# Moving deferred sums, row squares and a small rotary table to other places of a decoder-layer kernel

## The chip, the cores and the metric

One core of one Trainium2 chip runs the whole program. The metric is the device time of one execution in microseconds (us); lower is better. The kernel before took 886.24 us (median of 3 runs, 885.25 to 886.32).

## What is computed

One layer of a hybrid decoder. The input is a sequence of 2048 rows of 1024 numbers, with 16 learned "meta" rows put in front. The rows are normalised and projected to eight parts of 512 columns; half of the layer is a gated short convolution (four groups of 128 columns), half is chunked retention (four heads of 128 columns). The mixed result is projected back and normalised.

```python
hn = rms_norm(h, norm_g)
proj = jnp.einsum('bld,de->ble', hn, w_in)
cx, cb, cc, cg, q, k, v, rg = jnp.split(proj, N_PROJ, axis=-1)
conv_out = short_conv_branch(cx, cb, cc, conv_w) * jax.nn.silu(cg)
qf = rotary(q.reshape(shp), pos) * (RET_HEAD_DIM ** -0.5)
kf = rotary(k.reshape(shp), pos)
ret = head_group_norm(retention_chunkwise(qf, kf, vf), ret_norm_g)
ret_out = ret * jax.nn.silu(rg)
h = h + jnp.einsum('ble,ed->bld', jnp.concatenate([conv_out, ret_out], axis=-1), w_out)
```

The 16 meta rows matter only as the state with which a head's retention starts and as the first two inputs of a convolution.

## The kernel before, in words

The sequence is worked in two halves of 1024 rows (`r` = 0 and 1; here: first and second half), then comes the output projection, eight pairs of row tiles. A half consists of eight **units**: unit 0 to 3 are the retention heads (`head`, L623), unit 4 to 7 the convolution groups (`conv_group`, L530; the very first is `group_plain`). `UNITS` (L37) gives their order: 4, 0, 1, 2, 3, 5, 6, 7 in the first half, 0 to 7 in the second.

A unit makes two **quads** (`quad`, L210). A quad multiplies a 2 by 2 block matrix of weights with one of activations by seven products instead of eight (a Strassen form), and each product is 12 matmuls of 128x512, since every operand is split in a high and a low part (L104 on ScalarE casts the high part `wh`, L116 on VectorE subtracts to get the low part `wl`). The weight parts have three buffers each (`RING`), so the cast for a product can start when the product three before it has ended. Three copies on ScalarE (L228, tag `tc`, four buffers) take partial results out of PSUM, after the products 0, 2 and 3; `copied[0]` names the last of them. GpSimd makes the sums of weight blocks (L138 to L141, shown under the helpers' lines L113 and L116).

A head's first quad gives its keys and values, the second its queries and gates. `rotary` (L583) turns keys and queries with four VectorE instructions, L587 to L590; `turned[0]` names the last of them. `meta_state` (L427) makes the head's starting state from the meta rows: it loads a 16 KB table `mr` (into the tag `tc`, L429 and L430), adds pairs of products (`meta_sums`, L421), turns them (L435 to L437), and multiplies on TensorE (L439). Scores, states and the group norm of a head (L695 to L767) run beside the next unit's first quad.

Activations also need sums of blocks. In the first half they are made on the way for the second half (`prepare`, L186, called with `load_x(1)`), in four steps; each step loads four 256 KB tiles of x, scales one on ScalarE (L180), makes three VectorE operations at L177 and a subtraction (L116, tile x), and stores four tiles to DRAM (`sums_x`, L193). In the second half four such steps make the sums of the output weights (`sums_w`; four VectorE subtractions at L116, tile w, and nothing on ScalarE). `MAKES_SUMS` (L39) lists the units after whose end a step is written down: 0, 1, 2, 5 and 0, 1, 2, 4. `row_factors` (L359) makes the row norms of the second half during the first: nine steps, eight of which load two tiles and square them on ScalarE (L336); after four, and after all eight, `spread_factors` (L338) turns the sums into a row in SBUF. Conv groups take four of these steps at their end (L930).

The order of instructions on each engine is not written by hand. The framework lays out the program by a planner that simulates time: of the instructions that are ready it takes the one written first in the program. Nothing is tied to the written place unless `tc.issue_after(ins)` says so: what the block writes for the same engine as `ins` is then queued behind `ins`. Each engine then works off its list in the order that the planner gave it; the DMAs stand in the list of SP.

Of the kernel before, what the change touches and what calls it, by code (L numbers as in the profile page):

```python
# [8 lines left out]
F32 = mybir.dt.float32  # L9
# [6 lines left out]
P = 128  # L16
D = 1024
SEQ = 2048
NMETA = 16
# [3 lines left out]
HB = 512  # L23
# [5 lines left out]
RING, RAW, GEN, COPIES = 3, 8, 16, 4  # L29
# [6 lines left out]

UNITS = (4, 0, 1, 2, 3, 5, 6, 7), (0, 1, 2, 3, 4, 5, 6, 7)  # L37

MAKES_SUMS = (0, 1, 2, 5), (0, 1, 2, 4)  # L39


def retention_constants():
# [31 lines left out]
def hybrid_trunk(ctx: ExitStack, tc: tile.TileContext, t, out: bass.AP, chunk_decay):  # L74
# [5 lines left out]
    nc = tc.nc  # L80
# [343 lines left out]
        add(nc.vector, c, c, d)  # L424
        return a, c, b, d

    def meta_state(h, scratch):  # L427

        rot = sb.tile([P, HB], F32, name="mr", tag="tc", bufs=COPIES)[:NMETA, : 2 * P].rearrange("p (a c) -> p a c", a=2)  # L429
        nc.sync.dma_start(rot, t["rot_m"][h])  # L430
        k, v, a, b = meta_sums(scratch)
        half = P // 2
        lo, hi = slice(0, half), slice(half, P)
        for i, j in ((lo, hi), (hi, lo)):
            nc.vector.tensor_tensor(out=b[:, i], in0=k[:, j], in1=rot[:, 1, i], op=ALU.mult)  # L435
        nc.vector.tensor_tensor(out=a, in0=k, in1=rot[:, 0], op=ALU.mult)
        add(nc.vector, k, a, b)  # L437
        up = ps_misc()
        nc.tensor.matmul(up[:, :P], k, v, start=True, stop=True)  # L439
        nc.scalar.copy(out=state[h], in_=up[:, :P])  # L440
# [179 lines left out]
                while waiting[stage]:  # L620
                    waiting[stage].pop(0)()

    def head(h, r, m, rot_t, f, turning, blocks, ahead, first=(), between=()):  # L623


        between = iter(between)
        to_cross = []
        k, v, late = [None, None], [None, None], []
        tables = [rot_t[:, :, j * HB : (j + 1) * HB] for j in range(2)]

        def take(i, j, pp, c):
# [27 lines left out]
        def take(i, j, pp, c):  # L659
            d = gen("qg")[:, :HB]  # L660
            if i == 0:
                if c is None:
                    nc.scalar.copy(out=d, in_=pp)
                else:
                    add(nc.vector, d, pp, c)
                rotary(d, tables[j])
                q[j] = d
            else:
                if c is not None:
                    add(nc.vector, d, pp, c)  # L670
                    pp = d
                nc.vector.tensor_tensor(out=d, in0=pp, in1=f[0][:, j * HB : (j + 1) * HB], op=ALU.mult)
                sg[j] = d
# [15 lines left out]
        with tc.issue_after(copied[0].ins):  # L689
            join(1)  # L690
        next(between, lambda: None)()
        if blocks[1]:
            meta_state(h, blocks[1])
        blocks = ahead()
        states = [state[h]]  # L695
        vt = []
# [157 lines left out]
    for r in range(NR):  # L854
        f = factors[r]
        rot_t = sb.tile([P, 2, BLK], F32, name="rot_t", tag="rot_t", bufs=1)
        p0 = NMETA + r * BLK

        def load_tables():
            nc.sync.dma_start(rot_t, t["rot"][:, :, p0 : p0 + BLK])  # L860

        if r == 0:
            w = [None] * 4
            loads = w_loads(2 * NG)

            def begin(half):
                for n in (half, 2 + half):
                    w[n] = plain_part(n, loads[n], FIRST_W)

            m, b = moving(  # L870
                load_x(r), gain_of, {(0, 0): lambda: begin(0), (0, KH - 1): lambda: begin(1), (0, KT - 1): normalise_meta}
            )
            first = [[p for a, p in w]]
            blocks = None, meta_products([a for a, p in w])
            first.append(plain_parts(w_loads(2 * NG + 1)))
            load_tables()
            nc.sync.dma_start(cols, t["cols"])
            t3 = [a[:, i * HB : (i + 1) * HB] for a in (row_tile("t3", 1) for _ in range(2)) for i in range(2)]
            t1 = [brief("t1") if n < BRIEF else sb.tile([P, HB], F32, name="t1", tag="tc", bufs=COPIES) for n in range(KH)]
            for kt in range(KH):  # L880
                b11, b21, b12, b22 = (b[n * KH + kt] for n in range(4))
                block_sums(b11, b12, b22, b21, t1[kt], t3[kt], gain_of(kt), gain_of(KH + kt), nc.gpsimd)
                parts(m, 2, kt, b22)
                parts(m, 6, kt, b21)
            for _ in row_factors(0, f):
                pass
            nc.sync.dma_start(causal, t["causal"])
            nc.sync.dma_start(conv_w, t["conv_w"])
            nc.sync.dma_start(ret_g, t["ret_norm_g"])

            def late_parts():
                for i, held in ((3, t1), (4, t3)):
                    for kt in range(KH):
                        parts(m, i, kt, held[kt])

            between = ()
            later = prepare(load_x(1), sums_x, gain_of)
        else:
            m, b = moving(load_x(r), gain_of)
            first = [plain_parts(w_loads(0))]  # L900
            load_tables()
            prepared(m, sums_x, (1, 3))
            between = (lambda: prepared(m, sums_x, (0, 2)),)
            blocks = None, None
            later = prepare(load_w_out, sums_w)
        steps = row_factors(r + 1, factors[r + 1]) if r < NR - 1 else iter(())
        units = UNITS[r]
        turning = None
        special = (first, between)
        for n, unit in enumerate(units):  # L910
            following = units[n + 1] if n + 1 < len(units) else None
            rest = lambda: ahead(r, following, early=n == 0)
            if r + n == 0:
                blocks, completion = group_plain(unit - NG, m, f, blocks[1], first, late_parts, rest)
                special = (), completion
            elif unit < NG:
                if turning is None:
                    turning = [row_tile(name, 1 - r) for name in ("apart", "across")]
                blocks = head(unit, r, m, rot_t, f, turning, blocks, rest, *(special if unit == 0 else ()))
            else:  # L920
                if r == NR - 1 and following is None:
                    idle = sb.tile([P, 2, BLK], F32, name="held", tag="rot_t", bufs=1)
                    areas = [idle[:, 0], idle[:, 1], row_tile("held", 0), row_tile("held", 0)]
                    for i, a in enumerate(areas):
                        for j in range(2):
                            n, kt = 2 * (i // 2), i % 2 * 2 + j
                            held[n, kt] = a[:, j * HB : (j + 1) * HB]
                            nc.sync.dma_start(held[n, kt], sums_w[n, kt])
                blocks = conv_group(unit - NG, r, m, f, blocks, rest)
                for _ in range(4 - r):  # L930
                    next(steps, None)
            if unit in MAKES_SUMS[r]:
                next(later, None)

    m, b = moving(load_w_out)
    final_g = row_tile("final_g", 1)
# [41 lines left out]
```

## Time and profile before

| | us |
|---|---|
| median of 3 runs (885.25, 886.32, 886.24) | 886.24 |
| the profiled execution | 885.25 |
| its span, first to last instruction | 883.4 |
| TensorE busy in the span | 866.2 |
| VectorE busy | 715.5 |
| ScalarE busy | 472.1 |
| GpSimd busy | 397.8 |

The span is what the profiler saw; 1.85 us of the profiled execution lie around it. PE is TensorE's matmuls, PEld its weight loads, DVE VectorE, ACT ScalarE, POOL GpSimd, SP the queue that issues the DMAs. "DVE mk L435" is a VectorE instruction of line 435 that writes tile mk. A number in square brackets behind an instruction is how long its engine stood idle before it, and what ended the idle time.

### The profile page before, as it was taken

What the parts mean: (1) busy time and instruction counts of PE and PEld (TensorE: products, weight loads), DVE (VectorE), ACT (ScalarE), POOL (GpSimd) and SP (SyncE); (2) the same over time, 40 slices, a digit from 0 to 9 for tenths busy, and PEclk for the clock granted to TensorE, in tenths of its full rate; (3) what the DMA queues carried; (4) which work ended last, traced back from release to release, by engine and by line L of the source; (5) the groups of instructions that cost most, each with busy time, mean ns of one, the idle gap of its engine ahead of it and who ended that gap; (6) DMA issues with size and microseconds to landing.
All of it is one profiled execution on the core that took longest, in us unless ns stands there. A gap on an engine that the chain in (4) does not pass through costs nothing.

```text
span 883.4 us, 12729 instructions
## 1 busy us (share of the span) xinstructions
PE 866.2 (98%) x4279; PEld 711.1 (80%) x4279; DVE 715.5 (81%) x1176; ACT 472.1 (53%) x871; POOL 397.8 (45%) x291
## 2 busy tenths in 40 slices
PE   8999899999999999999999999999999999999996
PEld 5778787878888777888888888887888888788885
DVE  6888898979877866899989898787768699666764
ACT  8665437364655564746464645534334475545553
POOL 0554232314135554452233323254547455777873
PEclk9999999999999999999999999999999999999999
DMA  9713444343435552846345353346121493545432
GB/s 340 238 61 73 121 108 132 108 128 123 103 109 186 153 155 71 281 137 187 123 101 162 87 165 84 119 132 191 61 72 60 143 369 108 180 156 190 155 122 81
DMA packets 110033, 125.31 MB, mean 142 GB/s; under 512 B 41424, under 2 KB 58128, under 8 KB 109968
## 3 DMA queue, kind: packets, MB, share of 16 engines
q1 hardware_dynamic: 109968, 124.50, 45.6%
q8 instruction: 34, 0.56, 0.3%
q14 instruction: 31, 0.25, 0.1%
HBM read 90.92 MB, written 25.17 MB: 131 GB/s over the span
## 4 chain that ended last, share of the span: by engine, by line
PE 78%; DVE 11%; DMA 4%; issue 2%; ACT 2%; POOL 1%; SPq 1%; POOLq 0%; DVEq 0%; ACTq 0%
PE pj L221 64%; PE pj L277 7%; DVE wl L116 2%; PE ms L732 2%; PE ms L733 2%; PE ms L722 1%; DVE ml L116 1%; DMA w<-in_w_out 1%; PE ms L709 1%; DVE rot L588 1%; DMA mr<-in_rot_m 1%; DVE rot L587 1%; PE ms L412 1%; PE ms L700 1%; DVE x L177 1%
## 5 line engine op out<-in xcount | busy, mean ns | idle before, releaser
L221 PE MATMUL pj<-mh,wl 128*128 128x512 f32 x1008 | 398.5, 395 | 4.7 <-DVE wl L116 2.1
L221 PE MATMUL pj<-mh,wh 128*128 128x512 f32 x1008 | 393.1, 390 | 0.0
L221 PE MATMUL pj<-ml,wh 128*128 128x512 f32 x1008 | 392.9, 390 | 0.0
L104 ACT CAST wh<-ra 128x512 fp32r<-128x512 f32 x216 | 133.6, 619 | 257.4 <-PE pj L221 218.2
L221 PEld LDWEIGHTS pj<-mh,wl 128*128 128x128 f32 x1008 | 189.3, 188 | 48.6 <-ACT tc L228 3.6
L221 PEld LDWEIGHTS pj<-mh,wh 128*128 128x128 f32 x1008 | 189.2, 188 | 39.8
L221 PEld LDWEIGHTS pj<-ml,wh 128*128 128x128 f32 x1008 | 189.4, 188 | 38.1 <-issue 0.5
L116 DVE TENSOR_TENSOR wl<-ra,wh 128x512 fp32r<-128x512 f32 x216 | 184.6, 856 | 42.4 <-ACT wh L104 42.0
L116 POOL TENSOR_TENSOR ra<-ra 128x512 f32<-128x512 f32 x72 | 113.8, 1580 | 93.7 <-PE ms L412 58.1
L116 POOL TENSOR_TENSOR ra<-sa,ra 128x512 f32<-128x512 f32 x36 | 52.5, 1459 | 99.5 <-DVE wl L116 97.8
L113 POOL TENSOR_TENSOR sa<-ra 128x512 f32<-128x512 f32 x36 | 53.8, 1493 | 92.1 <-DMA ra<-in_w_in 32.4
L228 ACT COPY tc<-pj 128x512 f32<-128x512 f32 x108 | 62.5, 579 | 0.0
L277 PE MATMUL pj<-ml,mh 128*128 128x512 f32 x128 | 50.2, 393 | 0.1
L277 PE MATMUL pj<-mh,mh 128*128 128x512 f32 x128 | 49.9, 392 | 0.0
L277 PE MATMUL pj<-mh,ml 128*128 128x512 f32 x128 | 48.9, 399 | 0.1
L745 POOL TENSOR_TENSOR rp<-rs,neg_half 128x4 f32<-128x4 f32 x16 | 17.8, 1112 | 54.2 <-DVE rs L113 54.1
L537 POOL TENSOR_TENSOR c<-c,rr 128x512 f32<-128x512 f32 x14 | 27.6, 1968 | 24.3 <-DVE c L537 13.0
L795 DVE TENSOR_TENSOR yo<-pj,yo 128x512 f32<-128x512 f32 x32 | 21.9, 686 | 18.7 <-POOL yo L113 13.4
L797 ACT ACTIVATE rot<-yo 128x512 f32<-128x512 f32 x32 | 20.2, 630 | 31.1 <-DVE yo L795 30.7
L537 POOL TENSOR_TENSOR c<-c,tc 128x512 f32<-128x512 f32 x14 | 26.7, 1905 | 19.6 <-ACT tc L564 19.6
L800 POOL TENSOR_TENSOR z<-yo,final_g 128x512 f32<-128x512 f32 x16 | 26.9, 1681 | 16.5 <-DVE yo L795 16.5
L104 ACT CAST wh<-sa 128x512 fp32r<-128x512 f32 x36 | 22.1, 615 | 21.1 <-PE pj L221 21.0
(138 smaller groups left out, 1189.1 us busy)
## 6 DMA issues: line engine op xcount, KB each, us to landing
ra<-in_w_in SPq DMA_DIRECT2D x128, 256.0 KB, 2.8
x<-in_xT SPq DMA_DIRECT2D x48, 256.0 KB, 4.5
w<-in_w_out SPq DMA_DIRECT2D x32, 256.0 KB, 4.7
ra<-mixed SPq DMA_DIRECT2D x32, 256.0 KB, 3.0
yo<-in_x SPq DMA_DIRECT2D x32, 256.0 KB, 4.6
ra<-in_x SPq DMA_DIRECT2D x16, 256.0 KB, 3.2
mixed<-c SPq DMA_DIRECT2D x16, 256.0 KB, 2.7
sums_x<-x SPq DMA_DIRECT2D x16, 256.0 KB, 3.0
```

Of the source, the lines that this page charges most:

```text
L104: nc.scalar.copy(out=hi, in_=src)
L113: eng.tensor_tensor(out=out, in0=a, in1=b, op=ALU.add)
L116: eng.tensor_tensor(out=out, in0=a, in1=b, op=ALU.subtract)
L221: nc.tensor.matmul(bank, a[:, ks], b, start=first and kt == 0 and n == 0, stop=kt == KH - 1 and n == 2, skip_group_check=not first,)
L228: copied[0] = nc.scalar.copy(out=c, in_=bank)
L277: nc.tensor.matmul(banks[i], a[:, ks], b, start=half + kt + n == 0, stop=half == 1 and kt == KH - 1 and n == 2,)
L537: eng.tensor_tensor(out=out, in0=a, in1=b, op=ALU.mult)
L732: nc.tensor.matmul(o[:, cs], pm[:, cs], vt[j][:, cs], start=True, stop=False)
L745: nc.gpsimd.tensor_tensor(out=rp, in0=rs, in1=neg_half.rearrange("p (c a) -> p c a", a=1), op=ALU.pow)
L795: last[0] = nc.vector.tensor_tensor(out=y, in0=pp, in1=y, op=ALU.add)
L797: nc.scalar.activation(junk, y, AF.Square, accum_out=ss[:, i, j : j + 1])
L800: nc.gpsimd.tensor_tensor(out=ys[i][j], in0=y, in1=final_g[:, j * HB : (j + 1) * HB], op=ALU.mult)
```

## The change

Three things move. The steps that make block sums go one unit on: they belong to heads 1, 2, 3 and conv group 6 in the first half, and heads 1, 2, 3 and conv group 5 in the second; in a head they are written behind the join of the values, ahead of the meta rows' part, the next unit's weight loads and the scores, and are queued on VectorE behind the turn of the first half of the queries; in a conv group, the squares and the sums are queued on ScalarE behind the last copy of the unit's second quad. The row squares go in five steps to a conv group of the first half instead of four. The table `mr` gets a buffer of its own and is loaded when the head begins, and `meta_state` is queued behind the queries too.

```diff
-MAKES_SUMS = (0, 1, 2, 5), (0, 1, 2, 4)
+MAKES_SUMS = (1, 2, 3, 6), (1, 2, 3, 5)
...
-    def meta_state(h, scratch):
-
-        rot = sb.tile([P, HB], F32, name="mr", tag="tc", bufs=COPIES)[:NMETA, : 2 * P].rearrange("p (a c) -> p a c", a=2)
+    def meta_table(h):
+        rot = sb.tile([P, 2, P], F32, name="mr", tag="mr", bufs=1)[:NMETA]
         nc.sync.dma_start(rot, t["rot_m"][h])
+        return rot
+
+    def meta_state(h, scratch, rot):
+
         k, v, a, b = meta_sums(scratch)
...
-    def head(h, r, m, rot_t, f, turning, blocks, ahead, first=(), between=()):
+    def head(h, r, m, rot_t, f, turning, blocks, ahead, sums, first=(), between=()):
...
-        to_cross = []
+        to_cross, queried = [], []
         k, v, late = [None, None], [None, None], []
+        rot = meta_table(h) if blocks[1] else None
...
                 rotary(d, tables[j])
+                queried.append(turned[0])
                 q[j] = d
...
         next(between, lambda: None)()
+        with tc.issue_after(queried[0].ins):
+            next(sums, None)
         if blocks[1]:
-            meta_state(h, blocks[1])
+            with tc.issue_after(queried[0].ins):
+                meta_state(h, blocks[1], rot)
         blocks = ahead()
...
-                blocks = head(unit, r, m, rot_t, f, turning, blocks, rest, *(special if unit == 0 else ()))
+                sums = later if unit in MAKES_SUMS[r] else iter(())
+                blocks = head(unit, r, m, rot_t, f, turning, blocks, rest, sums, *(special if unit == 0 else ()))
...
                 blocks = conv_group(unit - NG, r, m, f, blocks, rest)
-                for _ in range(4 - r):
-                    next(steps, None)
-            if unit in MAKES_SUMS[r]:
-                next(later, None)
+                with tc.issue_after(copied[0].ins):
+                    for _ in range(5 - r):
+                        next(steps, None)
+                    if unit in MAKES_SUMS[r]:
+                        next(later, None)
```

## Rows read from the trace of the kernel before

**Rows 1.** The page: busy time of engines; GpSimd's commonest operation (count, busy, mean ns).
```profile
PE 866.2 (98%) x4279; PEld 711.1 (80%) x4279; DVE 715.5 (81%) x1176; ACT 472.1 (53%) x871; POOL 397.8 (45%) x291
...
L116 POOL TENSOR_TENSOR ra<-ra 128x512 f32<-128x512 f32 x72 | 113.8, 1580 | 93.7 <-PE ms L412 58.1
```

**Rows 2.** Timeline of PE: matmuls with idle time before them (start, duration).
```profile
94.12 0.45 PE L439 MATMUL ms<-mk 16*128 16x128 f32 x2 [1.10 <-DVE mk L113]
...
107.24 0.47 PE L221 MATMUL pj<-mh,wl 128*128 128x512 f32 x1 [1.20 <-DVE wl L116]
...
118.47 0.49 PE L732 MATMUL ms<-v,pm 128*128 128x128 f32 x2 [0.98 <-DVE pm L724]
...
216.04 0.49 PE L732 MATMUL ms<-v,pm 128*128 128x128 f32 x2 [0.88 <-DVE pm L724]
...
288.73 0.50 PE L221 MATMUL pj<-mh,wl 128*128 128x512 f32 x1 [1.43 <-ACT tc L228]
...
295.09 0.50 PE L221 MATMUL pj<-mh,wl 128*128 128x512 f32 x1 [0.58 <-DVE tc L113]
...
596.36 0.47 PE L221 MATMUL pj<-mh,wl 128*128 128x512 f32 x1 [0.37 <-DVE wl L116]
...
599.88 0.47 PE L221 MATMUL pj<-mh,wl 128*128 128x512 f32 x1 [0.52 <-DVE wl L116]
```

**Rows 3.** Waits of DVE (total us, times, longest).
```profile
DVE mk L435 <- DMA mr<-in_rot_m: 11.2, 4, 4.1
```

**Rows 4.** Busy time by stretch (start:end, length, then PE, PEld, DVE, ACT, POOL).
```profile
92.50:120.50 28.00, 24.72 (x159) 20.02 (x158) 27.53 (x46) 12.36 (x25) 8.04 (x6) 1.00 0.46 134
...
191.30:214.40 23.10, 23.10 (x145) 18.84 (x144) 22.81 (x37) 12.99 (x26) 8.23 (x5) 1.00 0.47 150
...
251.00:265.00 14.00, 14.00 (x80) 12.19 (x79) 8.24 (x17) 6.26 (x12) 3.98 (x3) 1.00 0.28 84
```

**Rows 5.** Timeline of DVE, end of head 0: table wait, meta sums, a step of sums.
```profile
92.51 0.35 DVE L435 TENSOR_TENSOR mk<-mk,mr 16x64 f32<-16x64 f32 x2 [2.34 <-DMA mr<-in_rot_m]
...
104.15 0.47 DVE L113 TENSOR_TENSOR mk<-mk 16x128 f32<-16x128 f32 x2
...
105.76 0.73 DVE L177 SCALAR_TENSOR_TENSOR x<-x,gain 128x512 f32<-128x512 f32 x1
106.42 0.67 DVE L116 TENSOR_TENSOR wl<-ra,wh 128x512 fp32r<-128x512 f32 x1
...
109.55 0.67 DVE L116 TENSOR_TENSOR x<-x 128x512 f32<-128x512 f32 x1
```

**Rows 6.** Timeline of SP and DVE, head 1: the queries' turn, DMA issues, sums.
```profile
138.24 0.68 DVE L590 TENSOR_TENSOR qg<-qg,rot 128x512 f32<-128x512 f32 x1
...
138.73 0.42 SPq L430 DMA_DIRECT2D mr<-in_rot_m  x1
...
145.86 1.91 SPq L376 DMA_DIRECT2D x<-in_xT  x4
...
153.24 1.47 DVE L177 SCALAR_TENSOR_TENSOR x<-x,gain 128x512 f32<-128x512 f32 x1 [0.24 <-ACT x L180]
```

**Rows 7.** Timeline of ACT, conv group 5 of the first half.
```profile
278.73 0.63 ACT L336 ACTIVATE n<-n 128x512 f32<-128x512 f32 x1 [2.67 <-DMA n<-in_x]
...
288.11 0.57 ACT L228 COPY tc<-pj 128x512 f32<-128x512 f32 x1
...
289.58 1.37 ACT L761 COPY apart<-across 128x1024 uint16<-128x1024 uint16 x1
...
293.01 0.61 ACT L104 CAST wh<-ra 128x512 fp32r<-128x512 f32 x1
...
300.54 0.63 ACT L564 ACTIVATE tc<-tc 128x512 f32<-128x512 f32 x1 [1.62 <-DVE tc L537]
```

**Rows 8.** The chain that ended last (start, us, what).
```profile
300.98 24.75 PE pj L221 x108
...
596.82 1.20 DVE w L116 x2
```

## The prediction, made before the changed kernel ran

> **What bounds the kernel.** I read the page first, for the engines' busy time, then TensorE's timeline for its idle times, then VectorE's waits, and then the chain and the busy time of the stretches around each idle time. TensorE is busy for 866.2 us of a span of 883.4 [rows 1], and in long stretches one matmul follows another every 24.75 / 108 = 0.229 us [rows 8]. So a change can win only where TensorE stands idle. Where this change is at work, between the start of head 0 and the output projection, I find eight idle times of a third of a microsecond or more that it can touch [rows 2]. Four belong to the heads of the first half: 1.10 + 1.20 + 0.98 + 0.88 = 4.16 us. Two belong to conv group 5 there: 1.43 + 0.58 = 2.01. Two fall between conv groups 4 and 5 of the second half: 0.37 + 0.52 = 0.89. Together 7.06 us, 0.8% of the run, which is the most that the change can win.
>
> Behind the four in the heads stands VectorE. From 92.5 to 120.5 us it is busy for 27.53 of 28.0 us and from 191.3 to 214.4 for 22.81 of 23.1 [rows 4]: it has a backlog, and at the end of each stretch TensorE waits for it. Each stretch begins just after VectorE stood still for the meta table: four waits, 11.2 us in all, the longest 4.1 [rows 3], the first 2.34 [rows 5]. The idle time at 94.12 waits for the meta rows' part itself, the other three for work that came late through the backlog [rows 2]. The two of conv group 5 come from ScalarE: it waited 2.67 us for the first tile to be squared, and the copy at 288.11 came after the squares [rows 7]; TensorE began at 288.73, when that copy was done [rows 2]. In the second half the sums' subtractions stand in the chain at 596.82 [rows 8], between the two idle times there.
>
> **The parts, costed.** The sum is made against the profiled execution, 885.25 us, which is 0.99 below the median of the runs.
>
> *The table gets its own buffer and is loaded at the head's start.* It removes four waits from VectorE, 11.2 us in all and up to 4.1 [rows 3]. Its four DMA issues of 0.42 us on SP [rows 6] move ahead of the head's weight loads and stores. That is 1.7 us on SP, spread over four heads; SP mostly stands waiting for a weight buffer there (138.73 to 145.86 holds 7 us, but few issues [rows 6]). I take 0; without that cover a weight load would be 0.42 us late. The buffer's next load waits until the head before has read it, a whole head earlier, so nothing waits behind it.
>
> *The meta part follows the queries.* Six short VectorE instructions per head. Two of them, the sums (0.47 us together [rows 5]), come out of the crowded stretch at the head's end and go to the next head, behind the turn of its first queries. Behind them wait the product on TensorE and the copy that gives the state, which the states need only when the next unit is under way. I take 0 for the wait and count the 0.47 as relief.
>
> *Head 0 loses its step of sums.* Three operations of 0.73 and one of 0.67 [rows 5] are 2.86 us of VectorE, and four loads, 1.91 us where they stand together, go from SP there [rows 6]. VectorE's backlog at the end of head 0 falls by 2.34 + 0.47 + 2.86 = 5.67 us. TensorE's idle time there is 1.10 + 1.20 + 0.98 = 3.28 us [rows 2], so all three should go. At the end of head 2 the step stays, but the wait of 4.1 us [rows 3], the one just before 191.3, goes against an idle time of 0.88: that goes too. **Heads: -4.16 us.** The other bound is 0, if something else is late at the same points; I take the full gain, since the relief is 1.7 and 4.7 times the idle time.
>
> *Heads 1 and 2 keep a step.* It is written earlier, but its first operation stood at 153.24 already, 15 us after the queries' turn at 138.24, because the loads were issued only at 145.86, behind the previous head's stores [rows 6]. The hold does not bind and the loads wait for the same buffers. I take 0. Bounds: the early place lets VectorE wait for x as it did for the table, up to 2.34 us a head (rival 3); no gain beyond what is counted.
>
> *Head 3 gets a step.* Its tail runs in conv group 5, where VectorE is busy for 8.24 of 14 us [rows 4]: 5.76 idle against 2.86 of work, so 0. If the cover is gone, at most 2.86.
>
> In this place the trace has two durations for one operation: 0.73 at 105.76 [rows 5] and 1.47 at 153.24 [rows 6]. I take 0.73 to 1.47, so 2.86 to 5.8 for a step, which the idle 5.76 just covers. [...]
>
> *Conv group 5: squares held behind the last copy.* The wait for the first tile (2.67 us) and the late copy go, and with them 2.01 us of TensorE. But the squares now stand in one block between the last copy and the next unit's first cast, which is written later. From the third product's end to the next unit's first product lie 36 matmuls, 36 x 0.229 = 8.2 us. In that time ScalarE must do, with durations of [rows 7]: a copy 0.57, a cast 0.61, two copies of 1.37, a Silu 0.63, the squares at 0.63 each, and the next unit's first cast 0.61; VectorE's part adds 0.67 [rows 5]. With 8 squares that is 10.9 us, with all 10 it is 12.1; if the planner lets the cast pass, nothing is late. So TensorE is late by 0 to 3.9, and the net is -2.01 to +1.9. I take 8 squares, as many as four steps had, since two more tiles must wait for buffers: 2.7 - 2.0 = **+0.7 us**.
>
> *Conv group 6.* Six squares, no copies of 1.37, and the step's scaling on ScalarE, not in the rows; taken as a cast: 0.57 + 0.61 + 0.63 + 6 x 0.63 + 0.61 + 0.61 + 0.67 = 7.5 us, under 8.2: 0. With the two spread copies (0.57 each) ahead of the cast it is 8.6: +0.4 at most. The fifth step adds no work; it makes the third conv group free of squares.
>
> *Second half.* Head 0 loses and head 3 gains a step; no idle time there to win or lose [rows 2]. Conv group 4 loses its step, with 0.89 us behind it; group 5 gets it, without a head's tail beside it. Bounds -0.89 and 0 (the same idle times one unit on); I take **-0.4**.
>
> Sum: -4.16 + 0.7 - 0.4 = -3.9 us: 885.25 becomes 881.4, and the median 886.24 becomes **882.3**. Bounds of this case: -4.16 - 2.01 - 0.89 = -7.1 (879.1), and -4.16 + 1.9 + 0.4 = -1.9 (884.4).
>
> **Rivals.** A change of under 0.2%, 1.8 us, can't be told from none by this measurement (the three runs lie within 1.07).
>
> 1. *ScalarE's block gives it back.* All ten squares are loaded by the last copy and the planner keeps written order: conv group 5 costs +1.9, group 6 +0.4, the second half wins nothing. -4.16 + 2.3 = -1.9: 884.4, at the edge of no change. For it: the squares are written first. Against it: ScalarE's idle time just before, from which the copies profit.
>
> 2. *The sums run beside GpSimd.* Each of the four operations waits out a whole GpSimd subtraction of 1.58 us [rows 1]: 2.86 + 4 x 1.58 = 9.2 us against 5.76 idle, in head 3's tail: 3.4 us late. -3.9 + 3.4: 885.7, no change. Against it: one operation of the step at 1.47 is the worst that rows show. [...]
>
> 3. *A wait for x takes the place of the wait for the table (slower).* In heads 1 to 3 the step is now the first thing behind the queries that is free to go. If the planner counts on the 256 KB tiles earlier than they land, as it did with the table, VectorE stands still for them at the same place, before the same crowded stretch. Head 0 shows the price of a wait of 2.34 us together with a step: 3.28 us of TensorE. Three heads of that are 9.84; with -4.16 gone and +0.3 elsewhere the sum is +6.0: 892.2. It decides above (4.16 - 0.3) / 3 = 1.3 us per head. For it: 11.2 us of such waits in four heads [rows 3]. Against it: in head 1 the step waited 0.24 us [rows 6] and its loads keep their place.
>
> 4. *The change doesn't do what it says.* The holds are inert in the heads, and the table's load is placed as late as before. Then only head 0's step counts: -1.20 - 0.98 + 0.7 = -1.5: 884.8.
>
> **How the numbers follow.** Chances: the forecast 0.55, rival 1 0.15, rival 2 0.08, rival 3 0.17, rival 4 0.05. A third of rival 1 falls below 884.4, so faster: 0.55 + 0.05 = 0.60; slower: 0.17; the same: 0.10 + 0.08 + 0.05 = 0.23. The likeliest case's own range is 880 to 884.4. The range that should hold 8 in 10 takes in the bound of -7.1 and rivals 1, 2 and 4 with the scatter of the runs: 879.0 to 887.5; it leaves out rival 3.
>
> **What would show it.** Right: VectorE never waits for the tile mr; TensorE's idle times at the ends of heads 0 and 2 (94.12, 107.24, 118.47 and 216.04 before) are gone; the L177 group starts in heads 1, 2 and 3 and conv group 6; ScalarE's first square in conv group 5 no longer waits for a DMA, and TensorE's idle time moves from inside the group to its end. Wrong: VectorE or ScalarE waits for x in heads 1 to 3 (rival 3); L177 above 1.5 us in head 3 (rival 2); an idle time of over 3 us where conv group 6 begins (rival 1); the wait for mr still there (rival 4). What else would make it wrong is an idle time on TensorE at a place where none stood before, since the planner lays out all engines anew.

## The result and the profile after

The changed kernel took **887.84 us** (median of 20 runs, 886.80 to 890.30) against 886.37 for the kernel before (20 runs, 885.03 to 888.03): a ratio of 1.0019, 95% interval 1.0012 to 1.0026. It is slower by about 1.5 us, just inside the 0.2% that the forecast called no change. The forecast was 882.3 us, with a range up to 887.5.

The profiled execution took 890.30 us, the highest of the 20; its span is 888.5. So I compare the two traces by stretches, not by their ends. Each kernel has 3408 recorded matmuls that write tile pj; I take the start of the n-th of them, less the start of the n-th in the kernel before, at seven places, and list by how much that difference grows in each stretch (us, places by the time of the kernel before). The kernels in the columns to the right are the experiments further down.

| stretch (us) | change | no hold | squares spread | hold alone | late spread | spread, later sums |
|---|---|---|---|---|---|---|
| 0 to 71, start | +1.67 | +0.02 | -0.60 | +0.38 | +0.75 | +0.40 |
| 71 to 292, heads, first part of conv group 5 | -5.02 | -2.97 | -5.03 | -1.35 | -5.02 | -5.02 |
| 292 to 334, end of conv group 5 | **+6.06** | -0.83 | -0.99 | +4.12 | +5.89 | -1.19 |
| 334 to 363, end of conv group 6 | **+1.23** | -0.37 | +0.26 | +0.44 | +0.45 | +0.22 |
| 363 to 575 | -0.03 | +0.02 | -0.06 | +0.61 | -0.02 | +0.01 |
| 575 to 673, conv groups 4, 5, second half | **+0.89** | +0.93 | +0.05 | +0.03 | +0.93 | +0.93 |
| 673 to 749 | +0.60 | -0.01 | +0.59 | -0.01 | -0.01 | +0.01 |

The first and the last line I take for scatter of single executions: the change and the kernel without holds give TensorE one and the same order of work up to about 280 us, and their start differs by 1.65; the last line is 0.6 or nothing, whatever the edit. Without these two lines the change stands at +3.1. Its profiled execution was 2.5 above its median, nearly all of it those two lines (2.27), and that of before was 1.1 below: 3.1 - 0.2 - 1.1 = 1.8, which fits the measured 1.5.

TensorE's timeline of the changed kernel shows where the terms lie; a row is start, duration, line, operation, and the idle time before it:

```profile
93.16 0.45 PE L442 MATMUL ms<-mk 16*128 16x128 f32 x2 [1.19 <-DVE mk L113]
...
297.48 2.07 PE L307 MATMUL ms<-rot,ones 128*128 128x512 f32 x2 [3.61 <-DVE rot L300]
...
299.70 0.80 PE L221 MATMUL pj<-mh,wl 128*128 128x512 f32 x1
300.29 0.63 PE L221 MATMUL pj<-ml,wh 128*128 128x512 f32 x1
300.72 0.63 PE L221 MATMUL pj<-mh,wh 128*128 128x512 f32 x1
...
349.61 0.47 PE L221 MATMUL pj<-mh,wl 128*128 128x512 f32 x1 [0.99 <-DVE wl L116]
...
601.24 0.50 PE L221 MATMUL pj<-mh,wl 128*128 128x512 f32 x1 [1.33 <-ACT tc L228]
...
642.77 0.47 PE L221 MATMUL pj<-mh,wl 128*128 128x512 f32 x1 [0.43 <-DVE wl L116]
```

Of the eight idle times of before [rows 2], those at 107.24, 118.47, 216.04, 288.73 and 295.09 are gone. From start to start an idle time costs 0.16 us more than its bracket says: in an unbroken row each matmul is listed as 0.39 us long and the next starts 0.227 us after its start (35 starts from 304.21 to 311.94), while the bracket counts from the listed end. The first four are 1.20 + 0.98 + 0.88 + 1.43 + 4 x 0.16 = 5.1, the -5.02 of the second stretch. The one at 94.12 is still there, 1.19 instead of 1.10. In their place stands one of 3.61 us at the end of conv group 5, one of 0.99 behind conv group 6, and 1.33 + 0.43 in the second half for 0.37 + 0.52.

The waits for the table are gone. The view of the tile mr lists its loads now from 20 us on, and nobody who waited for it:

```profile
L429 SPq DMA_DIRECT2D mr<-in_rot_m x4: 326/332/340, 20.3 to 187.2; - x4
...
who waited for it (us, times):
```

**Conv group 5.** SP's timeline, then ScalarE's (L336 are the squares, L770 the crossed copies, L104 the cast for the next unit, L567 the Silu):

```profile
273.00 5.36 SPq L335 DMA_DIRECT2D n<-in_x  x10
```

```profile
286.32 0.58 ACT L228 COPY tc<-pj 128x512 f32<-128x512 f32 x1
286.80 2.56 ACT L770 COPY apart<-across 128x1024 uint16<-128x1024 uint16 x2
289.23 1.07 ACT L418 COPY mk<-ms 16x128 f32<-16x128 f32 x4
290.20 0.63 ACT L336 ACTIVATE n<-n 128x512 f32<-128x512 f32 x1
...
295.73 0.61 ACT L336 ACTIVATE n<-n 128x512 f32<-128x512 f32 x1
...
296.34 1.12 ACT L104 CAST wh<-ra 128x512 fp32r<-128x512 f32 x2
```

All ten tiles were loaded from 273 us on and lay ready. Behind the last copy (286.32; before, the last copy stood at 289.10, right behind the one at 288.11 of [rows 7]) ScalarE made the crossed copies, the meta copies and ten squares in one unbroken block, 290.20 to 296.3; the cast for the next unit stood behind them. VectorE went on only then:

```profile
295.24 0.16 DVE L113 TENSOR_TENSOR ss<-ss 128x4 f32<-128x4 f32 x1 [0.57 <-ACT n L336]
...
296.74 0.69 DVE L300 TENSOR_TENSOR rot<-ident,rc 128x512 f32<-128x512 f32 x1 [0.92 <-POOL rc L293]
...
297.42 1.29 DVE L116 TENSOR_TENSOR wl<-ra,wh 128x512 fp32r<-128x512 f32 x2
```

Here is also what the forecast hadn't: the fifth step of squares brings the first spread (L300, then L307 on TensorE) into this place. And TensorE, after 3.61 us of idleness, ran more slowly: the granted clock was 0.65 and 0.67 in the two windows from 295 to 305 us, and 1.00 ahead of them and behind. The windows of the changed kernel (start:end, length, PE, PEld, DVE, ACT, POOL, then the granted clock):

```profile
290.00:295.00 5.00, 3.88 (x18) 2.87 (x16) 3.81 (x8) 4.99 (x17) 1.30 (x1) 1.00 0.33 100
295.00:300.00 5.00, 2.52 (x4) 0.98 (x5) 2.63 (x8) 3.35 (x10) 2.88 (x3) 0.65 0.18 54
300.00:305.00 5.00, 5.00 (x16) 3.92 (x16) 1.23 (x1) 1.94 (x5) 2.43 (x3) 0.67 0.33 92
305.00:310.00 5.00, 5.00 (x24) 4.13 (x23) 3.47 (x4) 1.22 (x4) 2.91 (x2) 1.00 0.05 17
```

From 300.29 to 303.28 us the matmuls start 0.43 us apart instead of 0.227; seven of them cost 7 x 0.20 = 1.4 us, the first one 0.25 more.

The spread's product at 297.48 was slow too, in the window with 0.65: its pair of matmuls took 2.07 us, where the kernel before has 1.12 at a granted clock of 1.00 (325 to 335 us).

```profile
329.96 1.12 PE L307 MATMUL ms<-rot,ones 128*128 128x512 f32 x2
```

### The profile page after: what moved, and what is told of

Read it like the earlier page. It is cut to its first block, busy times and chain, and to the rows that moved or that the text cites. A ratio compares the mean times of both kernels' runs of the same rounds, so it can differ in the third digit from the quotient of the medians.

```text
span 888.5 us, 12728 instructions
## 1 busy us (share of the span) xinstructions
PE 868.7 (98%) x4279; PEld 712.7 (80%) x4279; DVE 719.8 (81%) x1176; ACT 472.1 (53%) x871; POOL 396.3 (45%) x291
## 5 line engine op out<-in xcount | busy, mean ns | idle before, releaser
L104 ACT CAST wh<-ra 128x512 fp32r<-128x512 f32 x216 | 133.7, 620 | 266.9 <-PE pj L221 219.7
L116 DVE TENSOR_TENSOR wl<-ra,wh 128x512 fp32r<-128x512 f32 x216 | 189.1, 877 | 44.0 <-ACT wh L104 43.5
L540 POOL TENSOR_TENSOR c<-c,rr 128x512 f32<-128x512 f32 x14 | 25.3, 1806 | 34.2 <-DVE c L540 20.2
L104 ACT CAST wh<-sa 128x512 fp32r<-128x512 f32 x36 | 22.1, 614 | 24.6 <-PE pj L221 24.6
```

What stands on the lines that cost most here:

```text
L104: nc.scalar.copy(out=hi, in_=src)
L116: eng.tensor_tensor(out=out, in0=a, in1=b, op=ALU.subtract)
L540: eng.tensor_tensor(out=out, in0=a, in1=b, op=ALU.mult)
```

## The experiments

Every kernel was timed in five rounds beside the kernel before, and each ratio is against the runs of before on the same chip: 23 (median 886.47) for no hold, four steps, heads alone and table alone; 33 (885.99) for sums alone, the free meta part, three steps and the earlier hold; 15 (886.56) for the meta part's hold, the hold alone, the spread squares and the old place of the second half's sums; 15 (886.35) for the last two in this section.

**Are the conv groups' holds the loss?** In the change, the conv groups' steps without the hold:

```diff
-                with tc.issue_after(copied[0].ins):
-                    for _ in range(5 - r):
-                        next(steps, None)
-                    if unit in MAKES_SUMS[r]:
-                        next(later, None)
+                for _ in range(5 - r):
+                    next(steps, None)
+                if unit in MAKES_SUMS[r]:
+                    next(later, None)
```

> The changed kernel without the hold behind the last copy in the conv groups; five steps of row squares, the places of the sums and the heads' part stay. In the profile of the changed kernel TensorE stood idle 3.61 us at 297.48 for the product that spreads the row norms (L307), then ran at a granted clock of 0.56 up to 304; I put that at 3.61 + 1.21 (the product took 2.07 us, not 0.86) + about 1.4 (seven matmuls at 0.43 instead of 0.23 us) = 6.2 us. Theory A, the hold makes the squares late: without it the idle time goes, about 881.6 us, ratio to the kernel before 0.994 to 0.996. Theory B, the fifth step brings the spread product forward into conv group 5: it stands there without the hold too (even earlier), TensorE still waits for it 2 to 4 us, ratio 0.999 to 1.003.

Measured: 882.95 us, ratio 0.9961 (0.9948 to 0.9973). That is a hair above theory A's range and far below B's, and 0.0058 less than the change, some 5.1 us. The stretches say the same: +6.06 and +1.23 become -0.83 and -0.37. The squares go back among the other work, and with them the old idle time behind the late copy:

```profile
285.33 0.50 PE L221 MATMUL pj<-mh,wl 128*128 128x512 f32 x1 [1.50 <-ACT tc L228]
```

**Four steps with the hold** (`range(4 - r)` for `range(5 - r)` in the change), the eight squares of the forecast.

> The changed kernel with four steps of row squares to a conv group instead of five; the hold and all else stay. The first spread product then belongs to conv group 6. Theory A (the hold is the cost): the block of squares still stands between the last copy and the next unit's cast, TensorE waits 2 to 4 us at the end of conv group 5, ratio 0.999 to 1.003. Theory B (the fifth step is the cost): no idle time of over 1 us at the end of conv group 5, no fall of the clock, ratio 0.994 to 0.996.

Measured: 886.88 us, 1.0002 (0.9992 to 1.0012), as theory A has it. TensorE:

```profile
295.39 0.50 PE L221 MATMUL pj<-mh,wl 128*128 128x512 f32 x1 [2.46 <-DVE wl L116]
...
297.04 0.63 PE L221 MATMUL pj<-mh,wl 128*128 128x512 f32 x1
297.47 0.63 PE L221 MATMUL pj<-ml,wh 128*128 128x512 f32 x1
...
300.03 0.44 PE L221 MATMUL pj<-ml,wh 128*128 128x512 f32 x1
```

The forecast's block with 8 squares was 2.7 us late; 2.46 is what it came to. But again the matmuls fall to 0.43 us apart (granted clock 0.67 from 295 to 300 us), here some five matmuls after the idle time, and seven of them with the two at the edges cost 7 x 0.20 + 0.14 + 0.05 = 1.6 us that no term of mine held.

**The heads' part alone.** The change without holds, and in the conv groups everything as before, with the sums at (1, 2, 3, 5) and (1, 2, 3, 4):

```diff
-MAKES_SUMS = (1, 2, 3, 6), (1, 2, 3, 5)
+MAKES_SUMS = (1, 2, 3, 5), (1, 2, 3, 4)
...
-                with tc.issue_after(copied[0].ins):
-                    for _ in range(5 - r):
-                        next(steps, None)
+                for _ in range(4 - r):
+                    next(steps, None)
```

> Only the heads' part of the change: table in its own buffer and loaded at the head's start, meta part and sums behind the queries in heads 1 to 3; the conv groups as before (sums of the last step in conv group 5 and 4, four steps, no hold). If the heads' gain is what the two profiles show (three of four idle times gone, 1.18 us left in head 0): 4.16 - 1.18 = 3.0 us faster than before, ratio 0.996 to 0.9975. Rival: the heads' gain is given back behind them (head 3 now carries sums into conv group 5, which keeps its own squares and sums), ratio 0.999 to 1.001.

Measured: 882.27 us, 0.9951 (0.9938 to 0.9964), 4.3 us faster (3.2 to 5.5 by the interval), more than the 0.996 to 0.9975 that I expected. By the trace it is 3.06 + 3 x 0.16 = 3.5: in the heads three of the four idle times are gone and the first stays (1.18).

**The table alone** (the kernel before with a buffer for mr, loaded at the head's start; no hold, sums in place).

> The kernel before with the table's own buffer and early load alone; meta part, sums and squares stay where they were written. If the waits for the table (11.2 us of VectorE in four heads) are what makes the backlog, three or all of the heads' four idle times go: 3 to 4 us faster, ratio 0.9955 to 0.9965. If the step of sums at the end of head 0 makes it, only the 1.10 us at 94.12 go: ratio 0.9985 to 0.999.

Measured: 885.87 us, 0.9994 (0.9985 to 1.0002): no change that can be told. **The sums alone** (the heads' part with the table and the meta part as before):

> The heads' part without the table's: the sums go to heads 1 to 3 behind the queries, the table keeps its place in the copies' buffers and its late load, the meta part is not held; conv groups as before. The table's part alone gave 0.9994, both together 0.9951. If the step of sums at the end of head 0 is what TensorE waits for there, 1.20 + 0.98 = 2.2 us go and 1.10 + 0.88 stay: ratio 0.997 to 0.998. If the two simply add, this run has what the table's lacks: 3.7 us, ratio 0.9953 to 0.9963.

Measured: 884.09 us, 0.9977 (0.9968 to 0.9985). **The heads' part without the hold of the meta part:**

```diff
-            with tc.issue_after(queried[0].ins):
-                meta_state(h, blocks[1], rot)
+            meta_state(h, blocks[1], rot)
```

> The heads' part without the hold of the meta rows' part: the table is early and in its own buffer, so the planner is free to do the meta part as soon as its products are there. In head 0 TensorE stands idle 1.18 us for the held meta part (L442). If the hold only makes that wait, it goes, and the run is 1.2 us faster than with the heads' part whole: ratio to the kernel before 0.9930 to 0.9940. If the hold is what keeps the meta part out of the crowded ends of the heads, idle times return there: ratio 0.996 or above.

Measured: 885.51 us, 0.9996 (0.9987 to 1.0005). So with the table loaded early the one line of hold carries nearly the whole gain: 0.9951 with it, 0.9996 without. It is the early table that needs the hold, since the sums alone, with the late table and the meta part not held, keep 0.9977. VectorE in head 1 shows where the meta part goes, first without the hold, then with it:

```profile
143.86 0.68 DVE L116 TENSOR_TENSOR wl<-ra,wh 128x512 fp32r<-128x512 f32 x1
144.46 0.47 DVE L113 TENSOR_TENSOR mk<-mk 16x128 f32<-16x128 f32 x2
144.87 1.37 DVE L439 TENSOR_TENSOR mk<-mk,mr 16x128 f32<-16x128 f32 x1
146.17 0.34 DVE L438 TENSOR_TENSOR mk<-mk,mr 16x64 f32<-16x64 f32 x2
```

```profile
135.92 0.69 DVE L593 TENSOR_TENSOR qg<-qg,rot 128x512 f32<-128x512 f32 x1
136.52 0.47 DVE L113 TENSOR_TENSOR mk<-mk 16x128 f32<-16x128 f32 x2
136.92 0.27 DVE L439 TENSOR_TENSOR mk<-mk,mr 16x128 f32<-16x128 f32 x1
...
138.86 0.69 DVE L116 TENSOR_TENSOR wl<-ra,wh 128x512 fp32r<-128x512 f32 x1 [1.08 <-ACT wh L104]
```

With the hold the part runs right behind the queries' turn, where VectorE has idle time (1.08 us behind it). Without it the same part stands 8 us later, in the crowded end of the head, and TensorE waits there for pm, in head 1 and again in head 2 (1.21 us at 213.51):

```profile
162.88 0.49 PE L740 MATMUL ms<-v,pm 128*128 128x128 f32 x2 [1.20 <-DVE pm L732]
```

The kernel with the table alone has the same two waits (1.21 us each), and TensorE's matmuls there follow the same pattern: from 71 to 292 us it wins 0.39 us, this one 0.53. Beside an early table without a hold, the move of the sums wins nothing. The waits are the smaller part of the loss. From the 253rd to the 961st matmul of pj (about 71 to 278 us) the kernel without the hold takes 4.7 us longer than the held one, but its idle time there is 2.42 us against 1.18, only 1.2 more. Another 2.0 us lie in the order of TensorE's work: it makes the meta rows' products (L412) in three groups a head instead of two, and from their starts to the next start these take 6.5 us in all against 4.5. The rest, some 1.4 us, stays open.

**The hold of the meta part alone** (early table and hold, sums where they were, no hold in the conv groups).

> Only the meta rows' part is changed: the table is loaded when the head begins and the part is held behind the turn of the queries; the sums stay where they were before, and no conv group has a hold. Theory A (the hold of the meta part brings the gain, with the table early): 3 to 4 us faster, ratio 0.9955 to 0.9965, no idle time for pm in the heads. Theory B (the shift of the sums out of head 0 is needed as well): two idle times of about 1 us at the ends of heads 0 and 2 stay, ratio 0.998 to 0.9995.

Measured: 884.56 us, 0.9982 (0.9973 to 0.9991), in theory B's range, but not with B's two idle times: those at 107 and 216 are gone, the one for pm at the end of head 0 grew from 0.98 to 1.98. So the two parts roughly add up: 1.6 us from the meta part, 2.0 from the sums, 4.3 from both, which the intervals allow.

**The hold alone** in the kernel before, four steps.

```diff
-                for _ in range(4 - r):
-                    next(steps, None)
-            if unit in MAKES_SUMS[r]:
+                with tc.issue_after(copied[0].ins):
+                    for _ in range(4 - r):
+                        next(steps, None)
+                    if unit in MAKES_SUMS[r]:
+                        next(later, None)
+            if unit in MAKES_SUMS[r] and unit < NG:
                 next(later, None)
```

> The kernel before with the conv groups' holds alone, four steps of squares, nothing else moved. Theory A (the hold's cost does not depend on the heads; four steps with hold minus four steps without was 1.0002 against 0.9951): ratio 1.004 to 1.006, an idle time of 2 to 2.6 us at the end of conv group 5, one near 0.9 us at the end of conv group 6, and a granted clock under 0.8 behind the first of them. Theory B (the hold costs only together with the moved sums, in the place that they take): 0.999 to 1.001.

Measured: 889.75 us, 1.0040 (1.0027 to 1.0053), as theory A has it. TensorE, with a fall behind it again (granted clock 0.93 from 295 to 300 us, 0.73 from 300 to 305):

```profile
299.66 0.79 PE L221 MATMUL pj<-mh,wl 128*128 128x512 f32 x1 [3.24 <-DVE wl L116]
300.26 0.63 PE L221 MATMUL pj<-ml,wh 128*128 128x512 f32 x1
```

The wait is longer than the 2 to 2.6 us that I expected, and at the end of conv group 6 no idle time appears, against what I expected of it. The hold's cost doesn't hang on the heads.

**Fewer squares in the block**: the change with three steps a conv group (`range(3)`).

> The changed kernel with three steps of row squares to a conv group instead of five, held as there: six squares stand behind the last copy of conv group 5, against eight with four steps and ten in the changed kernel. If the price is the length of ScalarE's block (theory A made exact), TensorE's wait at the end of conv group 5, 2.46 us with eight squares, falls by two squares of 0.62 us to 1.2 us, and the run is about 1.2 us faster than with four steps: ratio to the kernel before 0.998 to 0.9995. If it is where the planner puts the spread product or the cast, whatever the number of squares, the wait stays at 2 us or more and the ratio at 1.000 or above.

Measured: 884.40 us, 0.9980 (0.9971 to 0.9989), at the lower end of what the block's length gave. The wait is 1.36 us, and here the granted clock stays at 1.00 (290 to 300 us):

```profile
293.69 0.50 PE L221 MATMUL pj<-mh,wl 128*128 128x512 f32 x1 [1.36 <-DVE wl L116]
```

This kernel leaves four squares and a spread to conv group 7, and between 363 and 575 us it loses 2.75 us, with idle times of 0.81 and 1.05 us at 403.50 and 410.28; the kernel with four steps loses 0.65 there. That the squares left over do it is not shown.

**The hold one copy earlier**: heads' part alone, with four steps and the sums held behind the second copy of the second quad instead of the last.

> The heads' part alone, as in the run with the heads only, and in the conv groups squares and sums held behind the second copy of the second quad (the one after product 2) instead of not at all. Unheld, squares stand before that copy and TensorE waits 1.53 + 0.63 us for it and what follows. If a hold is good as such and only its place was late, these 2 us go and no block stands before the next unit's first cast: ratio to the kernel before 0.992 to 0.994. If any hold makes a block that the next unit's cast has to wait for, TensorE waits at the end of conv group 5 for 1 us or more: ratio 0.995 to 0.998.

Measured: 886.86 us, 1.0010 (1.0001 to 1.0019), worse than either expectation. The block now stands ahead of the last copy, which TensorE waits for (1.52 us), then come 0.75 and 0.98, and 2.13 at the start of the second half. A block of eight squares costs on either side of the copy.

**The squares spread out**: the heads' part with no block at a conv group's end; the steps are written one by one inside the two quads of a conv group, behind their first and second copies. `quad` queues such a step behind its copy on ScalarE (`issue_after`), so these squares are held too, but two at a time.

```diff
-    def conv_group(g, r, m, f, blocks, ahead):
+    def conv_group(g, r, m, f, blocks, ahead, steps):
...
+        one = lambda: next(steps, None)
-        quad(stationary(blocks), m, take)
+        quad(stationary(blocks), m, take, (one, one))
...
-        quad(stationary(load_raw(w_loads(n))), m, take)
+        quad(stationary(load_raw(w_loads(n))), m, take, (one, one))
```

> The heads' part of the change without the conv groups' holds, and the row-square steps written one by one behind the first and second copies of both quads of a conv group (four places of two squares) instead of in a row behind the second quad. What is left in conv group 5 without any hold is an idle time of 1.53 + 0.63 us. Theory (the squares cost time only where several of them stand together ahead of a copy or a cast): that goes, ratio 0.992 to 0.994. Rival (ScalarE's work in conv group 5 is late however the squares lie, or the loads cannot come earlier): 0.995 or more, with an idle time of over 1.5 us in conv group 5.

Measured: **879.88 us, 0.9929** (0.9917 to 0.9942), faster than both kernels. ScalarE makes the squares in pairs between copies and casts:

```profile
281.25 0.58 ACT L228 COPY tc<-pj 128x512 f32<-128x512 f32 x1
281.73 0.63 ACT L336 ACTIVATE n<-n 128x512 f32<-128x512 f32 x1
...
282.36 0.62 ACT L336 ACTIVATE n<-n 128x512 f32<-128x512 f32 x1
...
283.54 0.62 ACT L104 CAST wh<-ra 128x512 fp32r<-128x512 f32 x1 [0.47 <-PE pj L221]
```

and TensorE has no idle time from 270 to 300 us (the row of the windows, 30.00 of 30.00):

```profile
270.00:300.00 30.00, 30.00 (x156) 23.33 (x155) 26.70 (x52) 19.02 (x39) 18.36 (x15) 1.00 0.70 213
```

**The later place of the second half's sums**: the change without holds, with (1, 2, 3, 4) in the second half.

> The whole change without the conv groups' holds (five steps of squares as in the change), and in the second half the last step of sums after conv group 4, as in the kernel before. Theory (the holds are the whole loss and the later place of the second half's sums costs about 1 us): ratio 0.9945 to 0.9955, a little faster than the change without holds (0.9961). Rival (the place in the second half is nothing, the whole gain is that of the heads): 0.996 as there.

Measured: 881.55 us, 0.9946 (0.9934 to 0.9959), as the theory has it, but its interval overlaps that of the change without holds. The reverse edit, the spread squares with the change's places (1, 2, 3, 6) and (1, 2, 3, 5), was to tell:

> The heads' part and the squares spread over the quads as in the run before with that name, but the last steps of sums in conv group 6 of the first half and conv group 5 of the second, as in the change (there without a hold). Theory (the later place costs the second half about 1 us): ratio 0.9935 to 0.9945. Rival (its cost in the change comes from the hold, the place is nothing): 0.9925 to 0.9933, with idle times for wl between conv groups 4 and 5 of the second half gone or moved one unit on at the same size.

Measured: 880.68 us, 0.9933 (0.9920 to 0.9945). That is the upper edge of the rival's range, just below the theory's, and it can't be told from the 0.9929 with the old places. The traces can tell: +0.89 to +0.93 between 575 and 673 us in each of the four kernels of the table with the later place, with a hold or without, and 0.03 to 0.05 in the two with the old place. So the place costs 0.9 us, not the hold.

**Five steps, but both spreads behind all squares** (conv group 6), everything else as in the change:

```diff
-            f[2].append(spread_factors(ss, *(a[:, j * HB : (j + 1) * HB] for a in f[:2])))
+            todo.append((ss, [a[:, j * HB : (j + 1) * HB] for a in f[:2]]))
+            if r == 0 or j == 1:
+                for ss, rows in todo:
+                    f[2].append(spread_factors(ss, *rows))
+                todo = []
```

> The change as it is, five steps of squares and the hold, but the second half's two spreads both stand behind all sixteen squares, in conv group 6. Theory (the spread product, queued on TensorE ahead of the next unit's first product, is what five steps cost above four): with the squares' block ending near 296.3 us the first product can begin near 298.1 instead of 299.7, an idle time of about 4 us for wl at the end of conv group 5, followed by a clock fall; 1 to 1.6 us less than the change, ratio 0.9998 to 1.0007. Rival (the two more squares cost it, and the second spread now burdens conv group 6): 1.0015 to 1.0035.

Measured: 887.53 us, 1.0009 (1.0000 to 1.0018), between the two. The idle time is what I expected:

```profile
297.24 0.80 PE L221 MATMUL pj<-mh,wl 128*128 128x512 f32 x1 [4.12 <-DVE wl L116]
297.84 0.63 PE L221 MATMUL pj<-ml,wh 128*128 128x512 f32 x1
...
302.53 0.43 PE L221 MATMUL pj<-mh,wl 128*128 128x512 f32 x1
```

but eleven matmuls now start 0.43 us apart (granted clock 0.58 from 295 to 300 us, 0.74 from 300 to 305), and conv group 5 costs +5.89 against +6.06: the spread was not what made it dear, ten squares ahead of the cast were. The 0.8 us that this kernel has less lie at the end of conv group 6 (+0.45 against +1.23). There my theory of the spread fell. Why the end of conv group 6 is cheaper here, where both spreads now stand, is taken up below.

## Why the prediction was wrong

**What bounds the kernel**: right. Every gain and loss is an idle time of TensorE, or a clock that fell behind one.

**Heads, forecast -4.16 us.** Three of the four idle times went, 3.5 us by the trace; timed alone the part is worth 4.3 (3.2 to 5.5), so the size stood. The reasons stood only in part. The table's own buffer, to which I gave 2.34 of the 5.67 us of relief in head 0 and all of it in head 2, shows no gain by itself (0.9994). Worth 2.0 us are the sums out of head 0, and the rest comes from the hold of the meta part, for which I took "0 for the wait" and 0.47 us of relief: not a delay but an earlier place, in VectorE's idle time, and with it another order of TensorE's products. And the idle time at 94.12 stayed, because the same hold puts head 0's meta part behind the queries' turn, in VectorE's backlog, and the product L442 waits for it. VectorE of the changed kernel there:

```profile
91.15 0.68 DVE L593 TENSOR_TENSOR qg<-qg,rot 128x512 f32<-128x512 f32 x1
91.76 0.47 DVE L113 TENSOR_TENSOR mk<-mk 16x128 f32<-16x128 f32 x2
...
92.74 0.28 DVE L113 TENSOR_TENSOR mk<-mk 16x128 f32<-16x128 f32 x1
```

**Conv group 5, forecast +0.7.** This is the step that failed, in its count and in a term that it lacks. The count: "I take 8 squares, as many as four steps had, since two more tiles must wait for buffers". All ten loads were issued from 273 us on, 17 us before the block began. With the real ten my own sum gave 3.9 us late; the kernel with the late spread shows 4.12, and eight squares gave 2.46 for my 2.7. The block was sized well and counted wrongly. Missing altogether was the price behind these idle times: the matmuls there at 0.43 us, 1.6 us with eight squares (behind 2.46 us) and 11 x 0.20 + 0.26 = 2.5 with ten (behind 4.12). There 4.12 + 2.5 - 0.74 (the last idle time of before, 0.58 + 0.16) = 5.9, the +5.89 of that stretch. In the change +6.06, less the 1.43 + 0.16 won ahead of it, make a net of +4.5.

The count alone is not the miss. With the eight squares that I took, the kernel with four steps still needed 886.88 us, 4.6 above the forecast, and the hold alone, with eight squares and the heads as before, cost 3.5 us by its ratio, where I had +0.7. Of the 7.0 us between the forecast's -3.9 and the trace's +3.1, conv group 5 holds 3.8, the second half 1.3, conv group 6 1.2 and the heads 0.7.

**Conv group 6, forecast 0, at most +0.4**: +1.23 in the change, +0.45 in the kernel with the late spread, although that one has both spreads here. I had costed ScalarE and one wl; on VectorE a spread's steps and the sums stand ahead of the next unit's wl, in both kernels. In the change two of the operations there took 1.49 us (L177, at 341.04) and 1.37 (L448, at 346.00), where the shortest of the same lines in that trace took 0.73 and 0.27. Whether that makes the difference of 0.8 us no run settles.

**Second half, forecast -0.4**: +0.9. The loss behind the old place does go, but a larger one appears at the same place: ScalarE's Silu waits for a VectorE product of 1.77 us, and the cast and the copy that TensorE needs stand behind it. Before, a cast and a copy stood ahead of the Silu (593.31 and 593.84), and the product took 0.68 us. The six kernels of the table show that the place costs 0.9 us; this chain is read from the traces and was not tested by a run of its own.

```profile
597.76 1.77 DVE L540 TENSOR_TENSOR tc<-tc,rr 128x512 f32<-128x512 f32 x1
```

```profile
599.57 0.63 ACT L567 ACTIVATE tc<-tc 128x512 f32<-128x512 f32 x1 [4.38 <-DVE tc L540]
600.10 0.60 ACT L104 CAST wh<-ra 128x512 fp32r<-128x512 f32 x1
600.61 0.58 ACT L228 COPY tc<-pj 128x512 f32<-128x512 f32 x1
```

The sum of the trace: -3.5 + 4.5 + 1.2 + 0.9 = +3.1, what the table gives.

**The rivals.** Rival 1 named the place and the mechanism, and its sign for an idle time of "over 3 us where conv group 6 begins" came; its price, 884.4, lacked the slower matmuls and the second half's loss and had 0.4 us for conv group 6. Rival 2 fell: the median L177 took 0.74 us, and the longest, 1.49, is not in head 3's tail (0.73 each, from 250.94 us) but at 341.04, where a GpSimd operation of 1.29 us had begun at 340.69; the 1.47 of before began while one of 1.42 us ran (152.73). But two more that began during GpSimd work took 0.74 and 0.73 (339.17 and 344.74), and a step that pays a whole GpSimd subtraction for each of its operations, as rival 2 supposed, shows in no row. Rival 3 fell: VectorE waits for no tile x in heads 1 to 3. Its sum was also off: +6.0 still counts the -4.16 that its words call gone; without them it is +10.1. Rival 4 fell: the table's waits are gone and the holds act, one with a gain and one with a loss.

## What to carry to other kernels

A hold is an order, and its worth depends on what it pulls ahead of what: behind the queries it put a short job into idle time (1 to 4 us won), behind the last copy it put a long one in front of the next unit's first cast (3.5 to 5 us lost). The fastest kernel here holds its squares too, two behind a copy. Before a block is held behind an instruction, count all that is ready to run in it, not what ran there before, and ask what is written after it on the same engine. Work that nobody waits for goes in small pieces into the gaps, and with an idle time of TensorE goes the price of slower matmuls behind it where the trace shows them, as it did here behind 2.46 to 4.12 us: 1.4 to 2.6 us more.

## What the runs showed of the hardware

The granted clock fell behind some idle times and not behind others. It stayed at 1.00 behind 1.36 us (three steps), 1.52 and 2.13 (the earlier hold) and 2.30 (the sums alone); behind 1.98 (the meta part's hold alone) the next matmuls of pj start 0.23 to 0.24 us apart as well. Behind 2.46 (four steps), 3.24 (the hold alone), 3.61 (the change, with the spread's product) and 4.12 us (the late spread) it fell, to 0.67, 0.73, 0.65 and 0.58 in the lowest window of 5 us, with 7, 5, 7 and 11 matmuls at 0.43 us. It was back at 0.99 or 1.00 in a following window in which TensorE was busy for 5.00 of 5.00 us. In the case of 2.46 us five matmuls still ran at 0.23 before the fall. These four idle times therefore cost 1.4 to 2.6 us on top of themselves; the 2.6 are 1.4 + 0.25 and the 0.95 that the spread's product took longer. Between three and four steps of squares the wait grows by 1.1 us and the stretch from 292 to 334 us by 3.3 (+0.06 against +3.33), of which 1.6 are the slower matmuls. The whole runs lie only 2.2 parts in a thousand apart, about 2 us, since the kernel with three steps loses more further on.
